# An output projection done in three parts instead of two, two of them beside attention

## The chip, the cores and the metric

The kernel runs on one core of a Trainium2 chip. The metric is the device time of one execution in microseconds (us). Engines are called by their names: TensorE (PE in the profile, its weight loads PEld), VectorE (DVE), ScalarE (ACT), GpSimd (POOL), and SyncE (SP), whose queue issues most of the transfers.

## The reference

Two layers of a hybrid backbone work on 256 context tokens and 1024 latent tokens of 1024 features. Each layer normalises its input, projects it into the inputs of four mixers (S5, mLSTM, differential attention, gated linear attention or GLA), joins their four outputs of 256 features, projects them, and adds the result to its input through a gate. An MLP with squared ReLU follows. In the second layer only the latent tokens go on.

```python
s5 = s5_mixer(zc[0], zl[0], p, need_ctx)
ml = mlstm_mixer(zc[1:6], zl[1:6], p, need_ctx)
da = diff_attention_mixer(zc[6:9], zl[6:9], p, layer_idx, need_ctx)
gl = gla_mixer(zc[9:14], zl[9:14], p, need_ctx)
mix_l = jnp.concatenate([s5[1], ml[1], da[1], gl[1]], axis=-1) @ p['w_out']
x_lat = x_lat + g1 * mix_l
hl2 = rms_norm(x_lat, p['norm2_g']) * (1.0 + sc2) + sh2
x_lat = x_lat + g2 * sq_relu_mlp(hl2, p['mlp_w1'], p['mlp_w2'])
```

The same is done for the context tokens in the first layer, with their own gates.

## The kernel before

Features lie on partitions and tokens in the free dimension. The 1280 tokens form three blocks: block 0 holds the 256 context tokens, blocks 1 and 2 hold 512 latent tokens each. Products of full precision are made of three matmuls (`mm3`, lines 1128 to 1130): both operands are split into a high and a low part, and high times high, high times low and low times high are summed. In each layer S5 and GLA run first, beside the input projections, and write their outputs to `mix_d` in DRAM, a buffer of four mixers by two row blocks of 128 features.

Then comes the attention stage. Three generators are interleaved by hand. `da_mix` is attention: per head and query tile, scores on TensorE (`daps`), their maxima and copies on VectorE (`das`, line 489), the exponential on ScalarE (line 500), the combination of two maps on VectorE (line 508), transposes (`dapt`) and value products (`dapo`) on TensorE. It has 372 steps in layer 0 and 340 in layer 1 (counted in the code: a latent head has 85, a head's context part 8). `ml_mix` is mLSTM, with 90 and 80 steps. `p_out` is the first part of the output projection: rows of S5 and GLA (`MIX[0]`), in pieces of 256 tokens, 8 output blocks m each, so 40 steps in layer 0 and 32 in layer 1. `both(da, 1, ml, 0.25)` takes one mLSTM step for every four attention steps, and `beside(..., po, 0.12)` gives the projection 0.12 steps for each attention step.

A step of `p_out` loads a piece of the layer's input (`xo`), takes 12 matmuls into one PSUM bank (`wop`), scales them by the gate on ScalarE (`pg`, line 1484), adds on GpSimd (line 1485) and stores the sum to `xn_d`. The weights are split once, in the first piece of tokens (lines 1459 to 1461), stored to `wsp` in DRAM, and loaded from there afterwards (`whl`, two buffers). `mix_parts` loads and splits the mixer outputs (`mr`, `mh`, `ml`). The banks of `wop` and of attention's transposes have the same tag in this stage, with two buffers.

In the tail, X is loaded from `xn_d`, and the rows of mLSTM and attention (`MIX[1]`) are projected block by block, 512 tokens at a time, in the order of `LAST`: blocks 1, 2, 0 in layer 0, and 1, 2 in layer 1. Each m takes 4 x 3 matmuls, then line 1530 adds the result to X on VectorE. Squares of X and their sums (`nsq` on ScalarE, `np` on TensorE) follow, and `norm_block` makes the MLP's input from three operations per feature block (lines 1212 to 1214). Then the MLP starts.

Of the kernel before, what the change touches and what calls it, by code (L numbers as in the profile page):

```python
# [12 lines left out]
F32 = mybir.dt.float32  # L13
F32R = mybir.dt.float32r
# [9 lines left out]
T = 1280  # L24
# [1073 lines left out]
BLK = [(0, 256), (256, 768), (768, 1280)]  # L1098
# [2 lines left out]
ZORD = ["dak1 dak2 daq1 daq2 s50 s51 ga glk glq glv glr0 glr1 dav mlk0 mlk1 mlq0 mlq1 mlv mlo".split(),  # L1101
        "s50 s51 dak1 dak2 daq1 daq2 ga glk glq glv glr0 glr1 dav mlk0 mlk1 mlq0 mlq1 mlv mlo".split()]
BANKS = dict(z="m", ada="o", nm="b", s5p="a", s5v="a", s5y="o", s5z="b", das="a", dat="b", das2="x", dao="p", gls="a", glo="b", mls="o", mlv="m", wo="m")
MIX = ((0, 3), (1, 2))
FIRST = ((0, 1, 2), (1, 2, 0))
LAST = ((1, 2, 0), (1, 2))
LAT_ONLY = {"mlq0", "mlq1", "daq1", "daq2", "glq", "mlo", "glr0", "glr1"}
# [16 lines left out]
def mm3_steps(pe, out, pairs):  # L1124

    n = len(pairs)
    for i, ((ah, al), (bh, bl)) in enumerate(pairs):
        pe.matmul(out, ah, bh, start=i == 0, stop=False)  # L1128
        pe.matmul(out, ah, bl, start=False, stop=False)  # L1129
        pe.matmul(out, al, bh, start=False, stop=i == n - 1)  # L1130
        yield 3 * out.shape[-1]


def mm3(pe, out, pairs):
    for _ in mm3_steps(pe, out, pairs):
        pass


def beside(main, filler, rate, guard=contextlib.nullcontext):

    credit = 0.0
    for c in main:
        credit += rate * c
        if credit > 0:
            with guard():
                while credit > 0:
                    credit -= next(filler, 1e9)
# [69 lines left out]
def both(a, na, b, nb):  # L1217

    ca = cb = 0.0
    for x in a:  # L1220
        yield x
        ca += 1
        while cb / nb < ca / na:
            next(b, None)
            cb += 1
# [44 lines left out]
def tile_hybrid_backbone(ctx: ExitStack, tc: tile.TileContext, io, out):  # L1270
    nc = tc.nc
    env = Env()
# [44 lines left out]
    def mod(l, part, s):  # L1317
        return mods[l][:, 8 * part:8 * part + 8, s]

    def pool(nm, side=None):  # L1320
        p = tc.tile_pool(name=nm, bufs=1, side=side, reuse_waits="tile") if side else tc.tile_pool(name=nm, bufs=1, reuse_waits="tile")
        return p, p.__enter__()

    def shut(p):
        p.__exit__(None, None, None)
# [42 lines left out]
    for l in range(L):  # L1368
# [8 lines left out]
        if l == 0:  # L1377

            npc, P = pool("nx0", "right")
# [28 lines left out]
        def put(i):  # L1408
            def cb(m, t, c0):
                (nc.sync, nc.scalar, nc.sync, nc.sync)[i].dma_start(mix_d[i, m, :, c0:c0 + t.shape[1]], t)  # L1410
            return cb
# [3 lines left out]
        if l == 0:  # L1415
            ready(("dak1",))
            spc, P = pool("s5p0")
# [17 lines left out]
        shut(wpc)  # L1435
        blocks = range(3) if need else range(1, 3)
        x_d = io["xT"] if l == 0 else xl_d
        xn_d = env.dram.tile([128, 8, T], F32, name=f"xn{l}", tag=f"xn{l}")
        xl_d = env.dram.tile([128, 8, T], F32, name=f"xl{l}", tag=f"xl{l}")

        def mix_parts(P, t0, n, z, w=512):

            mh = P.tile([128, 4, w], F32R, tag="mh", name="mh", bufs=1)
            ml_ = P.tile([128, 4, w], F32R, tag="ml", name="ml", bufs=1)
            for k in range(4):
                mr = env.wp.tile([128, 512], F32, tag="zst", name="mr", bufs=2)
                nc.sync.dma_start(mr[:, :n], mix_d[MIX[z][k // 2], k % 2, :, t0:t0 + n])
                nc.scalar.copy(mh[:, k, :n], mr[:, :n])
                nc.vector.tensor_tensor(ml_[:, k, :n], mr[:, :n], mh[:, k, :n].bitcast(F32), op=ALU.subtract)
            return [(mh[:, k, :n], ml_[:, k, :n]) for k in range(4)]  # L1450

        wsp = [env.dram.tile([8, 128, 2, 512], F32, name=f"wsp{z}{l}", tag=f"wsp{z}{l}") for z in range(2)]

        def out_proj(m, n, z, parts, first):

            w = env.wp.tile([128, 2, 512], F32R, tag="whl", name="whl", bufs=env.whl)
            if first:
                raw = env.wp.tile([128, 512], F32, tag="raw", name="raw", bufs=2)
                nc.sync.dma_start(raw.rearrange("p (i y) -> p i y", y=256), io["wo"][l, m].rearrange("p (i y) -> p i y", y=256)[:, MIX[z][0]:MIX[z][1] + 1:MIX[z][1] - MIX[z][0]])
                nc.scalar.copy(w[:, 0], raw)  # L1460
                nc.vector.tensor_tensor(w[:, 1], raw, w[:, 0].bitcast(F32), op=ALU.subtract)
                nc.sync.dma_start(wsp[z][m], w.bitcast(F32))
            else:
                nc.sync.dma_start(w.bitcast(F32), wsp[z][m])
            wh, wl = (w[:, i].rearrange("p (k c) -> p k c", k=4) for i in range(2))
            p = env.bank("wo", "wop")
            mm3(nc.tensor, p[:, :n], [((wh[:, k], wl[:, k]), parts[k]) for k in range(4)])
            return p[:, :n]

        def p_out(P):  # L1470

            w = 256
            for b in blocks:
                t0, t1 = BLK[b]
                for c in range(t0, t1, w):
                    n = min(w, t1 - c)
                    g1 = mod(l, 2, b == 0)
                    parts = mix_parts(P, c, n, 0, w)
                    for m in range(8):
                        x = P.tile([128, w], F32, tag="xo", name="xo", bufs=2)  # L1480
                        nc.sync.dma_start(x[:, :n], x_d[:, m, c:c + n])
                        p = out_proj(m, n, 0, parts, c == BLK[blocks[0]][0])
                        pg = P.tile([128, w], F32, tag="pg", name="pg", bufs=1)
                        nc.scalar.mul(pg[:, :n], p, g1[:, m:m + 1])
                        nc.gpsimd.tensor_tensor(x[:, :n], x[:, :n], pg[:, :n], op=ALU.add)
                        nc.sync.dma_start(xn_d[:, m, c:c + n], x[:, :n])
                        yield n / 256
# [3 lines left out]
        wpc, env.wp = pool("wpd")  # L1491
        env.whl = 2
        poc, P = pool(f"po{l}")
        po = p_out(P)
        da = da_mix(env, l, st, zd["dav"], io["da_lam"][l], 0.8 - 0.6 * math.exp(-0.3 * l), io["da_ng"][l], env.bones, put_da, need)
        mgc, MG = pool(f"mlg{l}", "right")
        mgates = ml_gates(env, l, MG, zd["gates"], io["ml_gb"][l], io["amask"], io["hsel"])
        ml = ml_mix(env, l, mgates, lambda i: zd[("mlq0", "mlq1", "mlk0", "mlk1")[i]], zd["mlv"], zd["mlo"], io["ml_cw"][l], io["ml_cb"][l],
                    io["ml_ng"][l], io["cmask"], put(1), need)
        beside((1 for _ in both(da, 1, ml, 0.25)), po, 0.12)  # L1500
        list(ml)
        shut(mgc)
        list(po)
        env.banks.update(BANKS)
        shut(ps2c)
        ps2c = banks(f"ps2{l}")
# [8 lines left out]
        for b in blocks:  # L1515
            n = BLK[b][1] - BLK[b][0]
# [3 lines left out]
        woc, P = pool(f"wo{l}", "right")  # L1520
        env.wp = P
        parts = None
        for i, b in enumerate(LAST[l]):
            n = BLK[b][1] - BLK[b][0]
            s = 1 if b == 0 else 0
            parts = parts or mix_parts(P, BLK[b][0], n, 1)
            g1 = mod(l, 2, s)
            for m in range(8):
                p = out_proj(m, n, 1, parts, i == 0)
                nc.vector.scalar_tensor_tensor(X[b][:, m], p, g1[:, m:m + 1], X[b][:, m], op0=ALU.mult, op1=ALU.add)  # L1530
            if i + 1 < len(LAST[l]):
                b1 = LAST[l][i + 1]
                parts = mix_parts(P, BLK[b1][0], BLK[b1][1] - BLK[b1][0], 1)
            norm_block(env, P, X[b], block_rstd(env, P, X[b], n), n, scl[l][:, 1, s], mod(l, 3, s), *H[b])
        shut(woc)
        env.wp = wp
# [4 lines left out]
        hdc, P = pool(f"hid{l}", "right")  # L1541
# [6 lines left out]
        def acc(nm):  # L1548
            turn[0] += 1
            env.banks["mlp"] = "mb"[turn[0] % 2]  # L1550
            return env.bank("mlp", nm)

        def split_side(src):
            for gen, every in side:
                if steps[0] % every == 0:
                    next(gen, None)
            steps[0] += 1
            return split_w(env, src, 1024)
# [8 lines left out]
        for g in range(32 // G):  # L1567
            hid = []
            for f in range(G):
                wh, wl = (w.rearrange("p (k c) -> p k c", k=8) for w in split_side(io["w1"][l, G * g + f]))  # L1570
                hhi = P.tile([128, T], F32R, tag="hhi", name="hidhi", bufs=G + 1)
                hlo = P.tile([128, T], F32R, tag="hlo", name="hidlo", bufs=G + 1)
                for b in blocks:
                    t0, t1 = BLK[b]
                    n = t1 - t0
                    p = acc("m1p")
# [9 lines left out]
            if g < 32 // G - 1:  # L1586
                for i in range(G):
                    wh, wl = w2(i, split_side)
# [3 lines left out]
            else:  # L1592
# [26 lines left out]
    for b in blocks:  # L1619
        t0, t1 = BLK[b]  # L1620
        n = t1 - t0
        y = block_rstd(env, P, X[b], n)
# [94 lines left out]
```

## Time and profile before

| | us |
|---|---|
| median of 3 runs | 3681.51 |
| lowest and highest | 3678.64, 3687.2 |
| profiled execution, its own time | 3686.26 |
| its span in the profile | 3684.5 |

The span is the time from the first to the last recorded instruction; 1.8 us of the execution lie around it. The mean granted TensorE clock over the span is 0.955 of full speed. TensorE is busy 3393.9 us of the span, VectorE 2228.0, ScalarE 1309.5 and GpSimd 448.6. Busy times of TensorE hold the modelled ends of pipelined matmuls, so they are read beside the spacing of their starts.

### The profile page before, as it was taken

To read this page: it belongs to the slowest core of one execution; us is meant where nothing else is said; L and a number is where in the kernel's file an instruction comes from. 1 tells how busy PE (TensorE), PEld (TensorE's weight loads), DVE (VectorE), ACT (ScalarE), POOL (GpSimd) and SP (SyncE) were. 2 spreads that over 40 slices of the span, in tenths; PEclk is the share of its full clock that TensorE was granted. 3 is DMA by queue.
4 is the path that set the end of the run, shared out by engine and by line. 5 is a ranking of instruction groups with operands and counts; after the bars stand their busy time and mean duration, and the time that the engine had idled before them with its cause. 6 is when DMAs were issued, how large, how long until landed. Compare 5 with 4: busy or idle time off the path is not lost. (4 is left out here: it accounts for less than half of the span.)

```text
span 3684.5 us, 55377 instructions
## 1 busy us (share of the span) xinstructions
PE 3393.9 (92%) x21282; PEld 2677.8 (73%) x21282; DVE 2228.0 (60%) x5455; ACT 1309.5 (36%) x2457; POOL 448.6 (12%) x520
## 2 busy tenths in 40 slices
PE   6989998898789999999999798988889899999998
PEld 3767767676657888888888476867677578888885
DVE  9664785878659855555544647486888543333334
ACT  4223434666542121212111522444776422122222
POOL 2131221223100000000000113130222000000000
PEclk8989999898899999999999898999999899999999
DMA  6775314655461222222111365314654511111112
GB/s 220 238 221 155 119 68 143 211 181 169 146 205 58 90 83 76 85 76 76 64 41 38 110 197 163 111 66 141 219 175 126 191 41 46 52 46 52 46 49 77
DMA packets 233966, 430.36 MB, mean 117 GB/s; under 512 B 47414, under 2 KB 135910, under 8 KB 233446
## 3 DMA queue, kind: packets, MB, share of 16 engines
q1 hardware_dynamic: 192806, 381.03, 31.7%
q10 hardware_dynamic: 35520, 30.52, 2.6%
q0 software_dynamic: 5376, 15.28, 1.2%
q8 instruction: 168, 2.75, 0.3%
q14 instruction: 96, 0.79, 0.1%
HBM read 316.88 MB, written 109.86 MB: 116 GB/s over the span
## 5 line engine op out<-in xcount | busy, mean ns | idle before, releaser
L1566 DVE SCALAR_TENSOR_TENSOR X<-m2p,mods,X 128x256 f32<-128x256 f32 (+1 forms) x512 | 344.9, 682 | 345.5 <-PE m2p L1130 344.9
L1119 ACT CAST whi<-raw 128x1024 fp32r<-128x1024 f32 x182 | 191.1, 1050 | 919.7 <-PE m2p L1129 640.8
L1128 PE MATMUL m2p<-hidhi,whi 128*128 128x512 f32 (+1 forms) x1280 | 473.4, 372 | 3.1 <-DVE X L1566 2.4
L1130 PE MATMUL m2p<-hidhi,wlo 128*128 128x512 f32 (+1 forms) x1280 | 472.0, 370 | 0.8 <-DVE wlo L1120 0.8
L1128 PE MATMUL m1p<-h2hi,whi 128*128 128x512 f32 (+1 forms) x1280 | 472.6, 370 | 0.2 <-ACT h2hi L1213 0.2
L1129 PE MATMUL m2p<-hidlo,whi 128*128 128x512 f32 (+1 forms) x1280 | 472.7, 369 | 0.0
L1129 PE MATMUL m1p<-h2lo,whi 128*128 128x512 f32 (+1 forms) x1280 | 471.0, 368 | 0.0
L1130 PE MATMUL m1p<-h2hi,wlo 128*128 128x512 f32 (+1 forms) x1280 | 470.9, 368 | 0.0
L1120 DVE TENSOR_TENSOR wlo<-raw,whi 128x1024 fp32r<-128x1024 f32 x182 | 224.5, 1234 | 315.2 <-ACT whi L1119 302.7
L1128 PEld LDWEIGHTS m2p<-hidhi,whi 128*128 128x128 f32 x1280 | 241.3, 189 | 60.4 <-issue 9.4
L1128 PEld LDWEIGHTS m1p<-h2hi,whi 128*128 128x128 f32 x1280 | 241.0, 188 | 46.5 <-ACT whi L1119 4.2
L1130 PEld LDWEIGHTS m2p<-hidhi,wlo 128*128 128x128 f32 x1280 | 241.0, 188 | 46.4 <-issue 3.4
L1129 PEld LDWEIGHTS m2p<-hidlo,whi 128*128 128x128 f32 x1280 | 241.4, 189 | 41.8 <-issue 2.2
L1129 PEld LDWEIGHTS m1p<-h2lo,whi 128*128 128x128 f32 x1280 | 241.2, 188 | 40.6 <-DVE h2lo L1214 0.6
L1130 PEld LDWEIGHTS m1p<-h2hi,wlo 128*128 128x128 f32 x1280 | 241.0, 188 | 40.2 <-issue 0.4
L1128 PE MATMUL zp<-hhi,whi 128*128 128x512 f32 (+1 forms) x664 | 254.5, 384 | 11.3 <-ACT zst L1241 9.6
L1129 PE MATMUL zp<-hlo,whi 128*128 128x512 f32 (+1 forms) x664 | 251.4, 379 | 8.6 <-DVE hlo L1209 8.2
L489 DVE TENSOR_SCALAR_CACHE_REDUCE das<-daps 128x512 f32<-128x512 f32 (+1 forms) x400 | 225.8, 587 | 45.5 <-PE daps L488 42.9
L1130 PE MATMUL zp<-hhi,wlo 128*128 128x512 f32 (+1 forms) x664 | 250.0, 377 | 0.0
L1580 DVE TENSOR_TENSOR rl<-rl,m1p 128x256 f32<-128x256 f32 (+1 forms) x160 | 100.6, 629 | 172.2 <-ACT rl L1579 172.1
L500 ACT ACTIVATE das<-das,danm 128x1280 f32<-128x1280 f32 x128 | 174.3, 1362 | 48.1 <-DVE danm L498 47.9
L488 PE MATMUL daps<-daqk,daqk 128*128 128x512 f32 (+1 forms) x400 | 149.7, 438 | 41.3 <-DVE das L489 39.8
(460 smaller groups left out, 6571.9 us busy)
## 6 DMA issues: line engine op xcount, KB each, us to landing
raw<-w SPq DMA_DIRECT2D x136, 512.0 KB
adaw<-ada_w SPq DMA_DIRECT2D x96, 512.0 KB
whl<-wsp SPq DMA_DIRECT2D x80, 512.0 KB
wsp<-whl SPq DMA_DIRECT2D x32, 512.0 KB
raw<-wz SPq DMA_DIRECT2D x30, 512.0 KB
daqk<-da_st SPq DMA_DIRECT2D x24, 640.0 KB
mlE<-ml_rows SPq DMA_DIRECT2D x16, 640.0 KB
xn<-xo SPq DMA_DIRECT2D x72, 128.0 KB
```

What stands on the lines that cost most here:

```text
L488: pe.matmul(p[:, 0:b - a], Q[m][:, 128 * qt:128 * qt + 128], K[m][:, a:b], start=True, stop=True)
L489: v.tensor_scalar(s[:, a:b], p[:, 0:b - a], -1.0, None, op0=ALU.mult, op1=ALU.min, accum_out=pm[:, i:i + 1])
L500: act.activation(s[:, :k1], s[:, :k1], AF.Exp, bias=nm[:, 0:1], scale=-1.0, accum_out=sm[m])
L1119: nc.scalar.copy(hi, raw)
L1120: nc.vector.tensor_tensor(lo, raw, hi.bitcast(F32), op=ALU.subtract)
L1128: pe.matmul(out, ah, bh, start=i == 0, stop=False)
L1129: pe.matmul(out, ah, bl, start=False, stop=False)
L1130: pe.matmul(out, al, bh, start=False, stop=i == n - 1)
L1566: nc.vector.scalar_tensor_tensor(X[b][:, m], p[:, :n], mod(l, 5, s)[:, m:m + 1], X[b][:, m], op0=ALU.mult, op1=ALU.add)
L1580: nc.vector.tensor_tensor(rl[:, :n], rl[:, :n], p[:, :n], op=ALU.mult)
```

## The change

The output projection is cut into three parts: `MIX` becomes (S5, GLA), (mLSTM), (attention). The first part runs beside attention and mLSTM, as before, at 0.2 steps per attention step, and mLSTM at 0.43; after `SPLIT` steps of attention (210 in layer 0, 190 in layer 1) what is left of mLSTM and of the first part is finished. The second part, mLSTM's rows with half as many matmuls per step, runs beside the rest of attention at 0.25. It reads the first part's sums from a new buffer `xm_d` and writes `xn_d`. The tail is left with attention's rows.

```diff
-MIX = ((0, 3), (1, 2))
+MIX = ((0, 3), (1,), (2,))
+SPLIT = (210, 190)
...
+        xm_d = env.dram.tile([128, 8, T], F32, name=f"xm{l}", tag=f"xm{l}")
...
         def mix_parts(P, t0, n, z, w=512):
+            nk = 2 * len(MIX[z])
...
-            for k in range(4):
+            for k in range(nk):
...
-        wsp = [env.dram.tile([8, 128, 2, 512], F32, name=f"wsp{z}{l}", tag=f"wsp{z}{l}") for z in range(2)]
+        wsp = [env.dram.tile([8, 128, 2, 256 * len(MIX[z])], F32, name=f"wsp{z}{l}", tag=f"wsp{z}{l}") for z in range(3)]
...
-            w = env.wp.tile([128, 2, 512], F32R, tag="whl", name="whl", bufs=env.whl)
+            nk = 2 * len(MIX[z])
+            w = env.wp.tile([128, 2, 512], F32R, tag="whl", name="whl", bufs=env.whl)[:, :, 0:128 * nk]
...
-            mm3(nc.tensor, p[:, :n], [((wh[:, k], wl[:, k]), parts[k]) for k in range(4)])
+            mm3(nc.tensor, p[:, :n], [((wh[:, k], wl[:, k]), parts[k]) for k in range(nk)])
...
-        def p_out(P):
+        def p_out(P, z, x_d, xn_d):
...
-        po = p_out(P)
+        po = [p_out(P, 0, x_d, xm_d), p_out(P, 1, xm_d, xn_d)]
...
-        beside((1 for _ in both(da, 1, ml, 0.25)), po, 0.12)
+        beside((1 for _ in itertools.islice(both(da, 1, ml, 0.43), SPLIT[l])), po[0], 0.2)
         list(ml)
         shut(mgc)
-        list(po)
+        list(po[0])
+        beside((1 for _ in da), po[1], 0.25)
+        list(po[1])
...
-            parts = parts or mix_parts(P, BLK[b][0], n, 1)
+            parts = parts or mix_parts(P, BLK[b][0], n, 2)
...
-                p = out_proj(m, n, 1, parts, i == 0)
+                p = out_proj(m, n, 2, parts, i == 0)
```

## Rows read from the trace of the kernel before

**Rows 1.** The page: busy us, share of the span, instructions.
```profile
PE 3393.9 (92%) x21282; PEld 2677.8 (73%) x21282; DVE 2228.0 (60%) x5455; ACT 1309.5 (36%) x2457; POOL 448.6 (12%) x520
```

**Rows 2.** Windows: us, busy PE, PEld, DVE, ACT, POOL, PE clock, DMA share, GB/s.
```profile
648.00:1002.00 354.00, 306.08 (x2606) 237.29 (x2605) 277.21 (x932) 229.02 (x514) 83.06 (x78) 0.90 0.53 174
...
1015.00:1105.00 90.00, 80.98 (x337) 49.91 (x338) 50.97 (x79) 38.11 (x65) 0.00 (x0) 0.97 0.60 204
2565.00:2874.00 309.00, 266.57 (x2284) 206.34 (x2286) 252.16 (x815) 212.78 (x445) 75.38 (x64) 0.91 0.55 179
...
2888.00:2953.00 65.00, 59.96 (x206) 35.01 (x206) 33.59 (x48) 24.62 (x40) 0.00 (x0) 0.93 0.55 182
```

**Rows 3.** Two windows of 30 us in layer 0's attention stage, same columns.
```profile
820.00:850.00 30.00, 18.48 (x171) 13.13 (x169) 23.89 (x68) 19.25 (x50) 10.32 (x5) 0.76 0.38 128
...
880.00:910.00 30.00, 29.23 (x267) 22.49 (x267) 23.99 (x89) 19.62 (x44) 10.16 (x8) 1.00 0.62 192
```

**Rows 4.** Waits, VectorE and SP, layer 0: us in total, times, longest us.
```profile
DVE das L489 <- PE daps L488: 27.7, 31, 3.0
...
SPq L1486 <- POOL xo L1485: 85.9, 35, 8.2
```

**Rows 5.** Line 1530 in either tail, and what it waited for (us, times).
```profile
L1530 DVE SCALAR_TENSOR_TENSOR X<-wop,mods,X x24: 476/750/752, 1017.8 to 1104.2; 128x512 f32<-128x512 f32 x16, 128x256 f32<-128x256 f32 x8
...
  PE wop L1130: 23.3, 13
...
L1530 DVE SCALAR_TENSOR_TENSOR X<-wop,mods,X x16: 744/750/752, 2890.4 to 2952.1; 128x512 f32<-128x512 f32 x16
...
  PE wop L1130: 22.4, 11
```

**Rows 6.** Timeline of VectorE in layer 0's tail: start us, us, what.
```profile
1043.84 0.75 DVE L1530 SCALAR_TENSOR_TENSOR X<-wop,mods,X 128x512 f32<-128x512 f32 x1 [1.97 <-PE wop L1130]
...
1051.16 1.28 DVE L1449 TENSOR_TENSOR ml<-mr,mh 128x512 fp32r<-128x512 f32 x2
...
1053.42 0.74 DVE L1530 SCALAR_TENSOR_TENSOR X<-wop,mods,X 128x512 f32<-128x512 f32 x1
...
1070.64 0.75 DVE L1530 SCALAR_TENSOR_TENSOR X<-wop,mods,X 128x512 f32<-128x512 f32 x1 [1.85 <-PE wop L1130]
1074.57 0.75 DVE L1530 SCALAR_TENSOR_TENSOR X<-wop,mods,X 128x512 f32<-128x512 f32 x1 [3.18 <-PE wop L1130]
```

**Rows 7.** Timeline of TensorE in layer 0's tail.
```profile
1021.04 0.40 PE L1129 MATMUL wop<-ml,whl 128*128 128x512 f32 x1
...
1024.47 0.39 PE L1129 MATMUL wop<-ml,whl 128*128 128x512 f32 x1
...
1070.54 1.04 PE L1187 MATMUL np<-nsq,ones 128*32 128x512 f32 x2
1071.51 0.50 PE L1128 MATMUL wop<-mh,whl 128*128 128x512 f32 x1
...
1090.06 0.28 PE L1130 MATMUL wop<-mh,whl 128*128 128x256 f32 x1
...
1092.10 0.28 PE L1129 MATMUL wop<-ml,whl 128*128 128x256 f32 x1
```

**Rows 8.** Groups by line and shape, layer 0's attention stage: busy us, mean ns.
```profile
L1484 ACT ACTIVATE pg<-wop,mods 128x256 f32<-128x256 f32 x40 | 18.8, 471 | 32.4 <-PE wop L1130 28.1 <-POOL xo L1485 3.9
...
L1449 DVE TENSOR_TENSOR ml<-mr,mh 128x256 fp32r<-128x256 f32 x20 | 8.0, 417 | 1.0 <-ACT mh L1448 1.0
```

**Rows 9.** Windows of the two attention stages, instructions of `wop` alone (PE, PEld, DVE, ACT).
```profile
648.00:1002.00 354.00, 80.98 (x480) 69.01 (x480) 0.00 (x0) 18.84 (x40) 0.90 0.53 174
...
2565.00:2874.00 309.00, 62.84 (x384) 54.46 (x384) 0.00 (x0) 15.08 (x32) 0.91 0.55 179
```

**Rows 10.** DMA issues in layer 0's attention stage: count, KB each.
```profile
X<-xn SPq DMA_DIRECT2D x2, 2048.0 KB
...
X<-xn SPq DMA_DIRECT2D x1, 1024.0 KB
```

More of the change, by code (lines that the diff above doesn't have):

```diff
@@ L4 @@
 import contextlib
+import itertools
 from concourse import mybir
@@ L1449, in mix_parts @@
                 nc.vector.tensor_tensor(ml_[:, k, :n], mr[:, :n], mh[:, k, :n].bitcast(F32), op=ALU.subtract)
-            return [(mh[:, k, :n], ml_[:, k, :n]) for k in range(4)]
-        wsp = [env.dram.tile([8, 128, 2, 512], F32, name=f"wsp{z}{l}", tag=f"wsp{z}{l}") for z in range(2)]
+            return [(mh[:, k, :n], ml_[:, k, :n]) for k in range(nk)]
+        wsp = [env.dram.tile([8, 128, 2, 256 * len(MIX[z])], F32, name=f"wsp{z}{l}", tag=f"wsp{z}{l}") for z in range(3)]
         def out_proj(m, n, z, parts, first):
-            w = env.wp.tile([128, 2, 512], F32R, tag="whl", name="whl", bufs=env.whl)
+            nk = 2 * len(MIX[z])
+            w = env.wp.tile([128, 2, 512], F32R, tag="whl", name="whl", bufs=env.whl)[:, :, 0:128 * nk]
             if first:
-                raw = env.wp.tile([128, 512], F32, tag="raw", name="raw", bufs=2)
-                nc.sync.dma_start(raw.rearrange("p (i y) -> p i y", y=256), io["wo"][l, m].rearrange("p (i y) -> p i y", y=256)[:, MIX[z][0]:MIX[z][1] + 1:MIX[z][1] - MIX[z][0]])
+                raw = env.wp.tile([128, 512], F32, tag="raw", name="raw", bufs=2)[:, 0:128 * nk]
+                nc.sync.dma_start(raw.rearrange("p (i y) -> p i y", y=256), io["wo"][l, m].rearrange("p (i y) -> p i y", y=256)[:, MIX[z][0]:MIX[z][-1] + 1:max(1, MIX[z][-1] - MIX[z][0])])
                 nc.scalar.copy(w[:, 0], raw)
@@ L1464, in out_proj @@
                 nc.sync.dma_start(w.bitcast(F32), wsp[z][m])
-            wh, wl = (w[:, i].rearrange("p (k c) -> p k c", k=4) for i in range(2))
+            wh, wl = (w[:, i].rearrange("p (k c) -> p k c", k=nk) for i in range(2))
             p = env.bank("wo", "wop")
-            mm3(nc.tensor, p[:, :n], [((wh[:, k], wl[:, k]), parts[k]) for k in range(4)])
+            mm3(nc.tensor, p[:, :n], [((wh[:, k], wl[:, k]), parts[k]) for k in range(nk)])
             return p[:, :n]
-        def p_out(P):
+        def p_out(P, z, x_d, xn_d):
             w = 256
@@ L1477, in p_out @@
                     g1 = mod(l, 2, b == 0)
-                    parts = mix_parts(P, c, n, 0, w)
+                    parts = mix_parts(P, c, n, z, w)
                     for m in range(8):
@@ L1481, in p_out @@
                         nc.sync.dma_start(x[:, :n], x_d[:, m, c:c + n])
-                        p = out_proj(m, n, 0, parts, c == BLK[blocks[0]][0])
+                        p = out_proj(m, n, z, parts, c == BLK[blocks[0]][0])
                         pg = P.tile([128, w], F32, tag="pg", name="pg", bufs=1)
@@ L1532, in tile_hybrid_backbone @@
                 b1 = LAST[l][i + 1]
-                parts = mix_parts(P, BLK[b1][0], BLK[b1][1] - BLK[b1][0], 1)
+                parts = mix_parts(P, BLK[b1][0], BLK[b1][1] - BLK[b1][0], 2)
             norm_block(env, P, X[b], block_rstd(env, P, X[b], n), n, scl[l][:, 1, s], mod(l, 3, s), *H[b])
```

## The prediction

> **What bounds the kernel now.** I read the page's busy shares first, then the windows, the waits, the groups by line and the timelines. TensorE is busy 92% of the span [rows 1], but most of that is input projection and MLP, which the change leaves alone. It works in two stretches of each layer, so those are read by themselves [rows 2]. The attention stage of layer 0 runs from 648 to 1002 us (354 us), of layer 1 from 2565 to 2874 (309 us). The tail, in which the second half of the output projection is done, carries on to 1105 and 2953: 90 us and 65 us after the last attention block has arrived.
>
> In the attention stage no engine is full. TensorE shows 306 of 354 us, VectorE 277, ScalarE 229; in layer 1 it is 267, 252 and 213 of 309 [rows 2]. TensorE's share overstates it: ends of matmuls are modelled, and of two windows of 30 us one has it at 29.2 and the other at 18.5, and VectorE works 24.0 and 23.9 in them [rows 3]. The longest wait of VectorE is for the score matmuls, 27.7 us over 31 times [rows 4], so the stage is a pipeline of three engines that take turns, VectorE the densest of those with honest durations: 0.783 of the stage in layer 0 and 0.816 in layer 1.
>
> In the tail it is plainer. VectorE works 51 of 90 us, and its update of X waits for the projection's matmuls 23.3 us over 13 times in layer 0 and 22.4 us over 11 times in layer 1 [rows 2, 5]. In steady state one output block m takes 3.93 us (X at 1070.64 and 1074.57) [rows 6]. That is 12 matmuls of 512 columns, 0.229 us apart (15 steps from 1021.04 to 1024.47), so 2.74 us, and 0.97 us of norm matmuls (1070.54 to 1071.51), 3.7 us together [rows 7]. The tail is TensorE's.
>
> **The change part by part.** (1) *Removed from the tail*: the two mLSTM row blocks, 6 of the 12 matmuls of each m. An m then costs 6 x 0.229 + 0.97 = 2.34 us, 1.37 less. VectorE needs about 2.2 us per m where X and the norm of the block before meet (three operations on 128x512, each taken at the 0.74 us of X [rows 6]), so TensorE and VectorE come out level and nearly all of the 1.37 us is real. Block 1 of layer 0: X runs from 1017.8 to 1043.84, seven periods of 3.72 us [rows 5, 6]; 7 x 1.37 = 9.6, less some 1.4 us because mLSTM matmuls of the first two m's are now done while the last attention block is still on its way: 8.2. Between blocks, X stands still from 1043.84 to 1053.42: four input pieces have to be split, in two pairs, the second only at 1051.16 [rows 6]. With two pieces that second pair is gone. Block 2 then needs its 8 x 2.34 = 19 us behind a shorter gap, but VectorE still has the norm of block 1 to do (from 1053.4, 16 operations and the X updates left over, about 14 us), so it ends near 1068 and not at 1079: 10 us rather than 14. The last block of 256 columns (0.12 us a matmul, 17 steps from 1090.06 to 1092.10 [rows 7]) is VectorE's more than TensorE's: 4 us. Layer 0: 22 us. Layer 1 has blocks 1 and 2 alone, at the same prices: 8 + 8 = 16. **Tail: -38 us.** Its upper end is every removed matmul at its spacing, 192 x 0.229 + 48 x 0.12 = 49.7 us; its lower end is half of what X waits for now, 23 us.
>
> (2) *Added to the attention stage*: 40 steps in layer 0 and 32 in layer 1. A step is 6 matmuls of 256 columns (0.12 us apart, 0.72 us), one scaling on ScalarE (0.471 us, 19 + 15 us in all), one add on GpSimd (its engine has 83 of 354 us, nothing waits), and three transfers on SP's queue: the x piece, the weight piece, and the store of the sum into the new buffer. Beside them stand 18 input splits (10 and 8, 0.417 us on VectorE) and 16 weight splits at half width, for which the 256-wide split is the nearest row [rows 8]. VectorE therefore gets 18 x 0.417 = 7.5 us in layer 0 and 16 x 0.417 = 6.7 in layer 1. At the density that the stage has now this is 7.5 / 0.783 + 6.7 / 0.816 = 17.8 us. **Stage: +18 us.** From below, nothing, if matmuls and splits fall into the gaps that exist. From above, the matmuls pay their whole place: at their issue spacing 432 x 0.12 = 52 us; at the busy time that a projection matmul shows in this stage now (81.0 us / 480 and 62.8 / 384, 0.169 and 0.164 us [rows 9]) 240 x 0.169 + 192 x 0.164 = 72 us. I take the VectorE figure because the stage waits around VectorE, and the room beside it (TensorE's weight loads fill 237 of 354 us [rows 2]) holds 29 us of matmuls.
>
> (3) *Moved*: the mLSTM steps go from 0.25 to 0.43 per attention step and the first part from 0.12 to 0.2, so both are over after 210 of the 372 attention steps (190 of 340 in layer 1); the rest of attention has only the second part beside it. The amount of work is unchanged, so I cost it at nothing; what hides it is that VectorE's density hardly moves between windows, whether mLSTM's heavy steps fall into them (820 to 850) or not [rows 3]. If that cover fails, the first stretch is the crowded one. SP already waits 85.9 us in the stage for the GpSimd add before it can issue a store [rows 4], with weight loads, key loads and decay rows queued behind; with the first part at 0.2 these come closer together.
>
> (4) *Late at the seam*: the final sum of the last 256 tokens is now stored at the very end of attention, where it used to be over 40 steps earlier. X is loaded from it in two pieces of 2 MB and one of 1 MB [rows 10]; one of 2 MB at the end delays the small loads of the last attention outputs on the same queue: +3 us, an estimate (0 to 12). A few adaptive-norm matmuls of the next layer that now lie in the tail move on into the MLP: +2 us.
>
> The rows show 0.229 us for 512 columns and 0.12 for 256 [rows 7], so cutting the mLSTM half into 256-wide pieces costs 5% more issue time: 52 us for what takes 49.7 in the tail. The Trainium skill, "Perfetto Trace Analysis", Optimizing Tensor Performance, speaks against this part: larger matmuls are more efficient than smaller ones where they are possible. The trace agrees, but only by those 2 us; the sum is the same by the rule and by the rows.
>
> **Sum**, against the profiled execution's own 3686.3 us (span 3684.5, 1.8 around it): -38 + 18 + 3 + 2 = -15, so 3671. That execution lies 4.8 us over the median of the runs, 3681.5; the median forecast is 3666 us.
>
> **Rivals.** *Full price in the stage.* TensorE is the stage's limit, as windows with 29.2 of 30 us suggest [rows 3]. Place: the issue slots of TensorE, in which the attention scores wait behind the projection. Then +52 for +18: -38 + 52 + 5 = +19, 3700 us. It decides from 33 us of stage cost on, where the tail's gain is gone. For it: VectorE's longest wait is for those scores [rows 4]. Against: weight loads fill only 67% of the stage.
>
> *All hidden.* The stage takes the new work for nothing: -38 + 5 = -33, 3648 us. For it: VectorE gets only 14 us. Against: three engines already take turns, and each new step occupies all of them. The Trainium skill, "Perfetto Trace Analysis", Identifying the Most-Contended Engine, says that matmul busy time is no measure of TensorE's room and that the weight-load share is; by it full price is out and VectorE is the engine to count, and the two rows of [rows 3] agree.
>
> *Gain eaten by the crowding.* The first stretch, with mLSTM and the first part pressed into 210 steps, loses another 15 us through SP's queue and buffers: net 0, 3681 us. For it: the SP wait [rows 4]. Against: the transfers average 174 GB/s at a DMA share of 0.53 in the stage [rows 2].
>
> **How the numbers follow.** The forecast (3650 to 3677) has 0.52, all hidden 0.15, crowding 0.13, full price 0.20. About 0.2%, 7 us, is what a measurement of this kernel can tell from no change, so faster is below 3674. Faster: most of the forecast (0.45) and all hidden, 0.60. Within: the forecast's upper edge 0.06, crowding 0.10, full price's lower edge 0.03, 0.19. Slower: 0.17 of full price, 0.03 of crowding and 0.01 of the forecast, 0.21. The range reaches from below all hidden (3638, tail near its upper end) to inside full price (3693).
>
> **What would show it.** Tail: X every 2.3 to 2.6 us instead of 3.9, no second pair of splits between blocks, first to last X in layer 0 down from 86 us to about 64. Stage: 18 us longer over both layers together, VectorE near 0.8 of it; TensorE's granted clock in it, now 0.90 and 0.91 [rows 2], not lower. Seam: the last X load behind the last attention store. I am wrong if the two stages grow by over 33 us, if VectorE's density falls in the first stretch, or if the tail's period stays above 3 us because a weight piece, with two buffers, arrives later than 2.3 us after its buffer is free.

## The result and the profile after

The changed kernel takes 3817.2 us (median of 4 runs, 3810.96 to 3832.17), the kernel before 3680.07 beside it: a ratio of 1.0375, 95% interval 1.034 to 1.0409. It is 137 us slower; 3666 was forecast, in a range that ended at 3693. Below, 1% is 36.8 us, and every ratio is against the kernel before run on the same chip.

The page of the changed kernel shows each engine with a little more work, to be compared with [rows 1].

```profile
PE 3447.9 (91%) x21474; PEld 2712.1 (71%) x21474; DVE 2242.0 (59%) x5479; ACT 1349.3 (35%) x2553; POOL 503.5 (13%) x592
```

No engine has more than 55 us added (GpSimd 55, TensorE 54, ScalarE 40, VectorE 14), so the 137 us are not the added work of any one of them. The windows tell where they lie (columns as in [rows 2]): first the two attention stages whole, each with its tail, then each stage cut where the second part begins.

```profile
648.00:1091.00 443.00, 362.52 (x2846) 279.89 (x2846) 293.29 (x948) 253.22 (x568) 112.02 (x116) 0.86 0.60 190
1095.00:1165.00 70.00, 57.46 (x214) 30.43 (x215) 46.93 (x75) 35.11 (x61) 0.00 (x0) 0.93 0.54 174
2630.00:3025.00 395.00, 325.15 (x2490) 246.97 (x2490) 264.95 (x836) 236.40 (x497) 95.29 (x96) 0.88 0.60 187
3030.00:3080.00 50.00, 42.90 (x124) 19.66 (x124) 30.26 (x46) 23.70 (x40) 0.00 (x0) 0.90 0.46 148
...
645.00:910.00 265.00, 226.07 (x1916) 179.33 (x1918) 189.63 (x619) 153.85 (x369) 78.42 (x74) 0.86 0.63 200
910.00:1091.00 181.00, 138.50 (x938) 101.92 (x938) 105.56 (x338) 101.32 (x207) 35.02 (x44) 0.86 0.57 177
...
2630.00:2880.00 250.00, 214.81 (x1732) 166.54 (x1732) 181.77 (x582) 152.63 (x338) 67.95 (x64) 0.86 0.61 195
2880.00:3025.00 145.00, 110.34 (x758) 80.43 (x758) 83.18 (x255) 83.76 (x159) 27.34 (x33) 0.90 0.56 174
```

The windows grew from 354 to 443 and from 309 to 395 us. They are cut by eye, so here are the last outputs of attention in layer 0 and layer 1, before and after (first and last start, us):

```profile
L556 DVE SCALAR_TENSOR_TENSOR dao<-dao,ng,rs_y x8: 340/700/746, 679.7 to 1005.7; 128x128 f32<-128x128 f32 x4, 128x512 f32<-128x512 f32 x4
L556 DVE SCALAR_TENSOR_TENSOR dao<-dao,ng,rs_y x4: 739/746/752, 2675.0 to 2881.9; 128x512 f32<-128x512 f32 x4
...
L557 DVE SCALAR_TENSOR_TENSOR dao<-dao,ng,rs_y x8: 339/542/752, 679.4 to 1091.1; 128x128 f32<-128x128 f32 x4, 128x512 f32<-128x512 f32 x4
L557 DVE SCALAR_TENSOR_TENSOR dao<-dao,ng,rs_y x4: 736/865/1046, 2768.5 to 3024.9; 128x512 f32<-128x512 f32 x4
```

The first score matmuls start at 648.1 and 2571.1 us before and at 645.8 and 2634.3 after. From there to the last output the stages grew by 87.7 and 79.8 us. VectorE worked 0.783 and 0.816 of the windows [rows 2]; now it is 293.29 / 443 = 0.66 and 264.95 / 395 = 0.67. It is 0.72 in the first stretch and 0.58 in the second of layer 0 (189.63 / 265, 105.56 / 181). No other engine took its place: TensorE and ScalarE are less dense too, and GpSimd works a quarter of the time. TensorE's granted clock is 0.86 and 0.88 in the two stages, where it was 0.90 and 0.91 [rows 2]. The tail did what was asked of it. These are the update of X in layer 0 and layer 1, answering to [rows 5]:

```profile
L1537 DVE SCALAR_TENSOR_TENSOR X<-wop,mods,X x24: 480/750/755, 1099.7 to 1162.8; 128x512 f32<-128x512 f32 x16, 128x256 f32<-128x256 f32 x8
...
  PE wop L1132: 13.0, 13
...
L1537 DVE SCALAR_TENSOR_TENSOR X<-wop,mods,X x16: 744/751/752, 3033.5 to 3076.8; 128x512 f32<-128x512 f32 x16
...
  PE wop L1132: 11.5, 8
```

From first to last X it takes 63.1 us in layer 0 (86.4 before) and 43.3 (61.7), and the waits for matmuls are halved. Stages and tails together make 87.7 + 79.8 - 23.3 - 18.4 = 125.8 us, and the spans of the two profiled executions differ by 124.7 (3809.2 against 3684.5). VectorE's timeline there answers to [rows 6]:

```profile
1099.71 0.75 DVE L1537 SCALAR_TENSOR_TENSOR X<-wop,mods,X 128x512 f32<-128x512 f32 x1 [1.31 <-PE wop L1132]
1100.99 0.75 DVE L1537 SCALAR_TENSOR_TENSOR X<-wop,mods,X 128x512 f32<-128x512 f32 x1 [0.20 <-PE wop L1132]
...
1116.47 0.75 DVE L1537 SCALAR_TENSOR_TENSOR X<-wop,mods,X 128x512 f32<-128x512 f32 x1 [0.61 <-PE wop L1132]
1117.14 1.28 DVE L1453 TENSOR_TENSOR ml<-mr,mh 128x512 fp32r<-128x512 f32 x2
...
1142.74 0.75 DVE L1453 TENSOR_TENSOR ml<-mr,mh 128x256 fp32r<-128x256 f32 x2
```

Between blocks there is one pair of splits, no longer two. So the loss is in the attention stage. In its second stretch (layer 0) these waits of GpSimd, VectorE and ScalarE are new or have grown (in the whole stage before, their totals were 6.8, 1.4, 6.4 and 3.9 us); columns are total us, times, longest:

```profile
POOL xo L1490 <- DMA xo<-xm: 64.3, 18, 8.0
...
DVE das L490 <- PE dapt L530: 21.8, 4, 8.8
...
DVE dao L551 <- ACT dao L550: 14.7, 2, 14.5
ACT pg L1489 <- POOL xo L1490: 11.9, 10, 2.0
```

GpSimd's timeline in the same stretch shows the adds of the second part:

```profile
1000.72 0.73 POOL L1490 TENSOR_TENSOR xo<-xo,pg 128x256 f32<-128x256 f32 x1 [4.34 <-DMA xo<-xm]
1002.67 0.73 POOL L1490 TENSOR_TENSOR xo<-xo,pg 128x256 f32<-128x256 f32 x1 [1.22 <-DMA xo<-xm]
...
1013.55 0.79 POOL L1490 TENSOR_TENSOR xo<-xo,pg 128x256 f32<-128x256 f32 x1 [4.36 <-DMA xo<-xm]
```

An add waits for its x piece, the one buffer of the scaled result waits for the add, ScalarE waits for that buffer, the PSUM bank for ScalarE, and attention's transposes, which use the same two banks, for the bank. That was the first theory (R): the second part's round trip through its buffers holds attention up. Its rival (P): the moved pacing costs by itself.

### The profile page after: what moved, and what is told of

Its sections match the earlier page's. It is cut to its first block, busy times and chain, and to the rows that moved or that the text cites. A ratio compares the mean times of both kernels' runs of the same rounds, so it can differ in the third digit from the quotient of the medians.

```text
span 3809.2 us, 56498 instructions
## 1 busy us (share of the span) xinstructions
PE 3447.9 (91%) x21474; PEld 2712.1 (71%) x21474; DVE 2242.0 (59%) x5479; ACT 1349.3 (35%) x2553; POOL 503.5 (13%) x592
## 5 line engine op out<-in xcount | busy, mean ns | idle before, releaser
L1130 PE MATMUL wop<-mh,whl 128*128 128x256 f32 (+1 forms) x512 | 183.1, 360 | 67.7 <-DMA whl<-wsp 29.4
L489 PE MATMUL daps<-daqk,daqk 128*128 128x512 f32 (+1 forms) x400 | 159.5, 464 | 45.6 <-DVE das L490 43.3
```

The lines of the kernel that those rows point to most:

```text
L489: pe.matmul(p[:, 0:b - a], Q[m][:, 128 * qt:128 * qt + 128], K[m][:, a:b], start=True, stop=True)
```

## The experiments

**The change taken apart.** The first pair splits the loss into three. One kernel has the new pacing and the old two parts:

```diff
-MIX = ((0, 3), (1,), (2,))
+MIX = ((0, 3), (1, 2))
...
-        beside((1 for _ in da), po[1], 0.25)
-        list(po[1])
+        list(da)
```

> The old two parts (S5 and GLA beside attention, attention and mLSTM in the tail), with the change's pacing (0.43, 0.2, SPLIT) and nothing beside the rest of attention. Theory R (the second part's round trip through its buffers holds attention up; the pacing is harmless): about the time of the kernel before, 3680 to 3705 us. Theory P (the pacing itself costs: mLSTM is the cover under which attention's waits lie, and the rest of attention is left without it): 3740 us or more, both stages longer by 30 us or more each with no second part in them, VectorE's busy share after 930 us of layer 0 below 0.5.

Measured: 3745.8 us, 1.0159 (1.013 to 1.0189). The other leaves the mLSTM part out of the changed kernel, so its output lacks that contribution:

```diff
-        po = [p_out(P, 0, x_d, xm_d), p_out(P, 1, xm_d, xn_d)]
+        po = [p_out(P, 0, x_d, xn_d)]
...
-        beside((1 for _ in da), po[1], 0.25)
-        list(po[1])
+        list(da)
```

> The changed kernel with the mLSTM part of the projection left out altogether (its output lacks mLSTM's contribution), everything else in place. Against the run with the pacing alone it shows the tail's gain by itself: both theories expect 30 to 45 us less than that run. Against the changed kernel it prices the second part: theory R expects 3650 to 3670 us, so that the second part costs 150 us; theory P expects 3710 to 3780, so that it costs 40 to 100.

Measured: 3713.54 us, 1.0077 (1.0054 to 1.0099). So the pacing costs 1.59% (58 us), the smaller tail gives 0.82% (30 us) back, and the second part costs 1.0375 - 1.0077 = 2.98% (110 us); the intervals of the three ratios are 8 to 13 us either way. Neither theory is enough alone: theory P has the total of the first run right and its place wrong. The windows of the run with the pacing alone:

```profile
645.00:940.00 295.00, 247.05 (x2096) 194.14 (x2097) 221.04 (x722) 173.28 (x404) 80.94 (x77) 0.88 0.62 201
940.00:1000.00 60.00, 52.78 (x384) 36.88 (x382) 54.34 (x176) 44.30 (x85) 0.00 (x0) 0.97 0.18 59
```

Attention by itself is not slow: VectorE works 54.34 of 60 us, 0.91, against 0.78 for the whole stage before. The time is lost in the first stretch, at 221.04 / 295 = 0.75. The Trainium skill, "Perfetto Trace Analysis", Optimization Strategy, says that where the most-contended engine changes over time, interleaving the regimes may help. The new pacing draws them apart, and that it cost 1.59% goes with the rule; but in the first stretch the rows show no engine that is full.

**The second part's waits.** Two edits to the changed kernel, one for each link of theory R. The second part's results go into the banks that mLSTM has left:

```diff
+        env.banks.update(wo="m")
         beside((1 for _ in da), po[1], 0.25)
```

> The changed kernel with the second part's PSUM results in the two banks that mLSTM has left, not in the two that it shares with the transposed attention weights. Theory R in the form that the shared banks tie attention to the second part's chain: 40 to 80 us faster than the changed kernel (3740 to 3775). If only the SP and GpSimd chain or the pacing matters: within 15 us of 3817.

Measured: 3786.93 us, 1.0278 (1.0258 to 1.0298), 0.97% or 36 us less than the changed kernel, a little under what theory R asked. The x pieces are loaded two steps ahead, and the scaled result gets a second buffer:

```diff
+        x = P.tile([128, w], F32, tag="xo", name="xo", bufs=4 if z else 2)
...
+    xs = [fetch(0), fetch(1)] if z else []
     for m in range(8):
+        if not z or m < 6:
+            xs.append(fetch(m + 2 * z))
+        x = xs.pop(0)
...
-        pg = P.tile([128, w], F32, tag="pg", name="pg", bufs=1)
+        pg = P.tile([128, w], F32, tag="pg", name="pg", bufs=2 if z else 1)
```

> The changed kernel with the second part's x pieces loaded two steps ahead into four buffers and two buffers for its scaled result, in the room that mLSTM has left. The 34 waits of GpSimd for that load (119 us in the whole run) should all but vanish. Theory R in the form that this load is the slow link: 40 to 90 us faster than the changed kernel (3730 to 3775). Theory P: within 20 us of it.

Measured: 3800.36 us, 1.0313 (1.0293 to 1.0333): 0.62%, 23 us. The waits for the piece are gone, as this row of its second stretch shows, but most of the time is not back:

```profile
POOL xo L1497 <- ACT pg L1496: 115.5, 36, 16.0
POOL xo L1497 <- DMA xo<-xm: 3.1, 1, 3.1
```

The bank is the dearer link. The Trainium skill, "Perfetto Trace Analysis", Optimizing Tensor Performance, asks that independent matmul groups rotate through PSUM banks so that eviction overlaps the next group; here two streams shared two banks, and separating them gave the 36 us. Both edits and four weight buffers together (the loosened kernel, below):

```diff
+        env.banks.update(wo="m")
...
+            w = (env.pq if z == 1 else env.wp).tile([128, 2, 512], F32R, tag="whl", name="whl", bufs=4 if z == 1 else env.whl)[:, :, 0:128 * nk]
```

> The changed kernel with everything of the second part loosened at once: results in the two banks that mLSTM left, x pieces loaded two steps ahead into four buffers, two buffers for the scaled result, four weight buffers. The second part costs 2.9% (110 us) in the changed kernel; the banks alone gave back 1.0%, the loads alone 0.6%. If its cost is waits (round trip and banks): 2.2% or more back, 1.010 to 1.018 of before, near the run without a second part (1.008). If it is work that the attention stage has no room for (TensorE issue, VectorE): 1.6% back or less, 1.022 or more.

Measured: 3767.89 us, 1.0226 (1.0195 to 1.0257). That is 1.49% (55 us) back, and as much of the second part's price is left. By the expectation that is the second outcome, work that finds no room; two runs below test it. First the round trip left out, all else as in the changed kernel (the output lacks mLSTM's contribution):

```diff
+                        if not z:
+                            x = P.tile([128, w], F32, tag="xo", name="xo", bufs=2)
+                            nc.sync.dma_start(x[:, :n], x_d[:, m, c:c + n])
...
+                        if not z:
+                            nc.gpsimd.tensor_tensor(x[:, :n], x[:, :n], pg[:, :n], op=ALU.add)
+                            nc.sync.dma_start(xn_d[:, m, c:c + n], x[:, :n])
```

> The changed kernel whose second part stops after the scaling: its x loads, GpSimd adds and stores are left out (the output lacks mLSTM's contribution), the weight and input loads, splits, matmuls, shared banks and scalings stay. If the round trip through DRAM, SP's queue and GpSimd carries the cost: 1.008 to 1.018 of before. If matmuls, banks and weight pieces carry it: 1.025 to 1.037.

Measured: 3781.55 us, 1.0277 (1.0252 to 1.0302): 0.98%, 36 us. So the round trip carries a third of the price, and matmuls, banks and weight pieces the rest. Is the rest TensorE's place? The loosened kernel with half of the second part's matmuls:

```diff
-            mm3(nc.tensor, p[:, :n], [((wh[:, k], wl[:, k]), parts[k]) for k in range(nk)])
+            mm3(nc.tensor, p[:, :n], [((wh[:, k], wl[:, k]), parts[k]) for k in range(1 if z == 1 else nk)])
```

> The loosened kernel (own banks, loads ahead, more buffers; 1.0226 of before, so that its second part costs 55 us) with 3 of the 6 matmuls of each step of the second part left out (half of mLSTM's contribution is missing). 216 matmuls are gone, 26 us at their issue spacing. If what is left of the second part's cost is TensorE's place: 20 to 30 us less, 1.014 to 1.017. If it is waits, transfers or VectorE: within 8 us, 1.020 to 1.025.

Measured: 3760.85 us, 1.0209 (1.0192 to 1.0226), 0.17% (6 us) under the loosened kernel, with intervals of 6 and 11 us either way. Most of their issue time of 26 us is not in it, so TensorE's work is at most a part of what is left. In the loosened kernel's second stretch TensorE does wait for its weights:

```profile
PEld wop L1130 <- DMA whl<-wsp: 7.3, 10, 1.5
PE wop L1130 <- DMA whl<-wsp: 6.8, 8, 1.7
```

The next run keeps the eight weight pieces in the room that mLSTM left, instead of storing them and loading them again for each piece of tokens (the expectation counts these loads too high: there are 32 in layer 0 and 24 in layer 1):

```diff
+            w = (env.pq.tile([128, 2, 256], F32R, tag="wk", name="whk", bufs=8) if first else env.kept[m]) if z == 1 else env.wp.tile(...)
```

> The loosened kernel (1.0226 of before) whose second part keeps its eight weight pieces in the room that mLSTM left, so that 64 loads of 256 KB a layer less eight first ones are gone (TensorE waited for such a piece 6.8 us in 100 us of the second stretch). If these loads are what is left of the second part's price: 0.7% or more less, 1.009 to 1.016. If the price is in the scalings and in engines that take turns: within 0.3%, 1.020 to 1.026.

Measured: 3749.11 us, 1.0165 (1.015 to 1.018): another 0.61% (22 us), most of what was expected if these loads were the rest. Over the kernel without a second part (1.0077) 0.88% is left, 32 us for 72 steps. With the stores moved to GpSimd's queue as well:

```diff
-                        nc.sync.dma_start(xn_d[:, m, c:c + n], x[:, :n])
+                        (nc.gpsimd if z else nc.sync).dma_start(xn_d[:, m, c:c + n], x[:, :n])
```

> The run before this one, with the second part's stores issued by GpSimd, right behind its own add, so that no load on SP's queue stands behind a store that waits for the add. If SP's order still holds the second part: another 0.5% or more less than with the weights kept alone. If not: within 0.3% of it.

Measured: 3751.09 us, 1.0176 (1.0154 to 1.0197), no gain. But the edit did not take the wait off SP. Between 930 and 1056 us SP had waited 43.1 us for the add and 11.6 us, before the next x load, for a store to leave its buffer; now it waits 68.9 us for the latter. Whether SP's order is a link is not told by this run.

**The pacing.** Two runs with the old two parts, one edit of the pacing each:

```diff
-        beside((1 for _ in itertools.islice(both(da, 1, ml, 0.43), SPLIT[l])), po[0], 0.2)
+        beside((1 for _ in both(da, 1, ml, 0.43)), po[0], 0.12)
```

> The old two parts, mLSTM at 0.43 steps per attention step as in the change, the first part at its old 0.12 over all of attention. The pacing alone cost 1.6% (58 us). Theory M (mLSTM pressed into 210 of 372 steps is what crowds the first stretch): 1.0% or more slower than before still, 3720 to 3745. Theory F (the first part at 0.2, its SP and GpSimd traffic, is what crowds it): within 0.4% of before.

Measured: 3721.62 us, 1.0111 (1.0096 to 1.0126).

```diff
+        beside((1 for _ in both(da, 1, ml, 0.25)), po[0], 0.2)
```

> The counterpart: mLSTM at its old 0.25, the first part at 0.2 beside all of it, old two parts. Theory M: within 0.4% of before (3670 to 3700). Theory F: 1.0% or more slower. If both runs lie near half, 0.6 to 1.0% each, it is the two together.

Measured: 3747.87 us, 1.0181 (1.0164 to 1.0198). None of the outcomes expected came: each pacing costs over 1% by itself, and the first part at 0.2 alone as much as the whole new pacing. The prices do not add up (1.1 + 1.8 against 1.6). A likely reason, which was not tried, is that the two together leave a stretch with attention alone, in which VectorE catches up (0.91 in the rows above). To see what the first part costs at 0.12, it was left out of the kernel before (its output lacks S5 and GLA):

```diff
-        po = p_out(P)
+        po = iter(())
...
-            nc.sync.dma_start(X[b], xn_d[:, :, BLK[b][0]:BLK[b][1]])
+            nc.sync.dma_start(X[b], x_d[:, :, BLK[b][0]:BLK[b][1]])
```

> The kernel before with its first part left out whole (the output lacks the S5 and GLA contribution); attention and mLSTM at their old 0.25, tail as it was. It prices the 72 steps of 12 matmuls that the attention stage carried already; at their issue spacing they are 104 us. If the stage has TensorE gaps that take projection work for little: 20 to 50 us less than before (0.986 to 0.995). If every projection matmul pays its whole place: 85 to 120 us less (0.967 to 0.977).

Measured: 3642.56 us, 0.9886 (0.9871 to 0.9901). At 0.12 the 72 steps cost 1.14%, 42 us, 0.58 us a step, where their matmuls alone take 1.44 us to issue: the stage does take them into its gaps. (The granted clock over the span was 0.941 to 0.945 without them and 0.955 to 0.958 in the kernel before beside it, so what the clock took is in the 42 us.) At 0.2 the same steps cost 1.0181 - 0.9886 = 2.95%, 109 us, 1.5 us a step. What makes density dear? Four runs, each with the first part at 0.2 and mLSTM at 0.25, and one thing taken from it. Its round trip (no x loads, adds, stores; X from the layer's input):

```diff
-                        x = P.tile([128, w], F32, tag="xo", name="xo", bufs=2)
-                        nc.sync.dma_start(x[:, :n], x_d[:, m, c:c + n])
...
-                        nc.gpsimd.tensor_tensor(x[:, :n], x[:, :n], pg[:, :n], op=ALU.add)
-                        nc.sync.dma_start(xn_d[:, m, c:c + n], x[:, :n])
```

> The kernel with the first part at 0.2 and mLSTM at its old 0.25 (1.018 of before), and the first part's round trip left out: no loads of x, no GpSimd adds, no stores of sums; X is loaded from the layer's input (the output lacks the S5 and GLA contribution). Weight pieces, input splits, matmuls and scalings stay. If the round trip through two x buffers and SP's queue is what makes a denser first part dear: 0.990 to 1.004. If it is the matmuls and their banks in between attention's: 1.010 to 1.018.

Measured: 3715.38 us, 1.0092 (1.0075 to 1.0109), 0.89% less. Between the two outcomes expected. The stores on GpSimd's queue, and the same edit to the kernel before as its control:

```diff
-                        nc.sync.dma_start(xn_d[:, m, c:c + n], x[:, :n])
+                        nc.gpsimd.dma_start(xn_d[:, m, c:c + n], x[:, :n])
```

> The first part at 0.2 and mLSTM at 0.25 (1.018 of before), with the stores issued by GpSimd. If a step's loads behind the store of the step before are what makes the denser first part dear: 0.7% or more less, 1.000 to 1.011. If it is the steps' work between attention's: 1.015 to 1.020.

> The kernel before, its first part's stores issued by GpSimd instead of SP; everything else as it was. SP waited 85.9 us for the add in the stage of layer 0. If SP's order costs time at the old density of 0.12 too: 0.4% or more faster than before (0.985 to 0.996). If the first part has slack there: 0.997 to 1.004.

Measured: 1.0203 (1.0186 to 1.022) and 1.0015 (1.0005 to 1.0024). No gain at either density. Here too the wait only moved. These are SP's waits in layer 0, ahead the two of the denser first part, then the one that is left with the stores moved:

```profile
SPq L1491 <- POOL xo L1490: 72.7, 37, 8.3
SPq L1486 <- DMA xn<-xo: 19.0, 14, 3.2
...
SPq L1486 <- DMA xn<-xo: 106.7, 28, 7.4
```

An x load needs the buffer that the store still holds, so it waits on SP in the store's place, 106.7 us for 91.7. The runs do not tell whether loads behind SP's waits make density dear. Half of the first part's matmuls:

```diff
-            mm3(nc.tensor, p[:, :n], [((wh[:, k], wl[:, k]), parts[k]) for k in range(nk)])
+            mm3(nc.tensor, p[:, :n], [((wh[:, k], wl[:, k]), parts[k]) for k in range(nk if z else 2)])
```

> The first part at 0.2 and mLSTM at 0.25, with 6 of the 12 matmuls of each step of the first part left out (GLA's contribution is missing); 432 matmuls, 52 us at their issue spacing. All transfers, splits, scalings and adds stay. If TensorE is what the dense stretch waits for: 0.8% or more less than 1.018, 1.000 to 1.010. If the weight pieces and the round trip are: 1.013 to 1.019.

Measured: 3731.91 us, 1.0141 (1.0117 to 1.0164): 0.40%, 15 us, for matmuls of 52 us issue time. The granted clock over the span fell beside it, from 0.947 to 0.949 to 0.940 to 0.943, so the 15 us are the matmuls' price less what the clock took. One weight piece for all steps, so no weight loads:

```diff
+            if z == 0 and not (first and m == 0):
+                w = env.one
```

> The first part at 0.2 and mLSTM at 0.25 (1.018 of before), with one weight piece, split once, used in all steps of the first part (its contribution is another matrix's). The weight loads, splits and stores of the first part are gone, 12 matmuls a step, input splits, scalings and the round trip of x stay. If the weight pieces make density dear: 1.000 to 1.009. If TensorE's place does: 1.013 to 1.019.

Measured: 3706.09 us, 1.0064 (1.004 to 1.0088): 1.17%, 43 us, the largest share. The splits and stores of seven weight pieces a layer went with the loads (on VectorE 14 x 0.69 = 10 us), and the granted clock rose to 0.954 to 0.957; both are in the 43 us. Windows of the same 120 us of layer 0: the kernel before, the denser first part, the denser first part with one weight piece, and the same without the round trip:

```profile
740.00:860.00 120.00, 103.38 (x897) 81.06 (x898) 96.62 (x317) 81.34 (x190) 28.48 (x29) 0.89 0.50 165
```

```profile
740.00:860.00 120.00, 110.69 (x908) 89.01 (x908) 80.18 (x267) 69.52 (x159) 30.41 (x32) 0.91 0.69 215
```

```profile
740.00:860.00 120.00, 105.57 (x929) 83.06 (x928) 95.20 (x299) 80.83 (x189) 34.51 (x34) 0.94 0.35 109
```

```profile
740.00:860.00 120.00, 114.94 (x1006) 92.99 (x1004) 78.99 (x273) 72.80 (x161) 10.95 (x13) 0.96 0.49 161
```

VectorE's work falls from 96.62 to 80.18 us and is 95.20 when the weight loads go, with 929 matmuls for 908; the DMA share goes 0.50, 0.69, 0.35. The share does not explain it: without the round trip it is 0.49, and VectorE has 78.99 us, in a kernel that is 0.89% faster. Nor does the granted clock, which is 0.89 in the kernel before and 0.91 with the denser first part. A window at fixed times also holds different steps in each kernel, so its density goes only roughly with the time. These are the weight loads in the same window of the kernel before and of the denser first part:

```profile
whl<-wsp SPq DMA_DIRECT2D x15, 512.0 KB
```

```profile
whl<-wsp SPq DMA_DIRECT2D x22, 512.0 KB
```

**Less dense on both sides?** The loosened kernel with its split after 290 (262) steps, mLSTM at 0.32, the first part at 0.145, the second at 0.5:

```diff
-SPLIT = (210, 190)
+SPLIT = (290, 262)
...
-        beside((1 for _ in itertools.islice(both(da, 1, ml, 0.43), SPLIT[l])), po[0], 0.2)
+        beside((1 for _ in itertools.islice(both(da, 1, ml, 0.32), SPLIT[l])), po[0], 0.145)
...
-        beside((1 for _ in da), po[1], 0.25)
+        beside((1 for _ in da), po[1], 0.5)
```

> The loosened kernel with the split later: mLSTM 0.32 and the first part 0.145 over 290 (262) attention steps, the second part at 0.5 beside the last 82 (78). If the pacing's 1.6% comes from the denser first stretch, it falls by more than half, and the second part's price stays near 55 us unless its own density costs in turn: 1.010 to 1.018. If the price rises with the density of projection steps wherever they stand, the second part gives the gain back: 1.020 to 1.030.

Measured: 3763.92 us, 1.0219 (1.02 to 1.0237), the same as the loosened kernel's 1.0226. What the first stretch gains, the second part, twice as dense, gives back: against the loosened kernel VectorE works 202.41 us for 194.01 between 645 and 910 us, and 99.58 for 116.95 between 910 and 1091. No version that does the whole computation beats the kernel before.

## Why the prediction was wrong

**The tail was right.** Step (1) gave -38; taken out alone the tail gave 30 us, from two ratios good to 8 and 11 us. The X spans shortened by 23.3 and 18.4 us where 22 and 16 were forecast (layer 1's second block was put at 8 and layer 0's at 10; at the same price layer 1 would have had 18). The period (2.39 us, seven of them from 1099.71 to 1116.47), the single pair of splits and the 64 us of layer 0 came as told. The seam of step (4), +5, was not measured by itself; it lies in the price of the second part.

**The step that failed first is (2), the stage at +18.** It counted the second part's matmuls, splits, scalings and adds, said of its three transfers only that they were on SP's queue, and of the add that nothing waits, though SP waits 85.9 us for it [rows 4] and ScalarE 3.9 [rows 8]. The part cost 110 us. 77 of them (1.0375 - 1.0165) went when its results had banks of their own, its loads ran ahead and its weights stayed, with all its matmuls, splits, scalings and adds still there. So they are not its arithmetic but the waits of a step that must fetch 256 KB of weights and 128 KB of x through two buffers every 3.7 us (38 x pieces between 940 and 1080 us). What is left, 32 us with the seam in it, lies within the bounds of the term, 0 and 52, but is nearly twice its 18; whether VectorE's density is its price is not shown. The step's waits had no price at all.

**The step that failed next is (3), moved work at nothing.** It cost 58 us. The cover named for it, VectorE's density hardly moving between windows, was read from two windows [rows 3] that both held projection steps at 0.12; it says nothing of windows with more. The text had the crowded first stretch as what is late if the cover fails, and as a rival at 15 us: the right place, at a quarter of its size. Whether it comes through SP's queue, as the text said, is open, for no run took SP's wait away.

**The rivals.** Full price was to be TensorE's issue slots. The total came out on its side, but its mechanism did not: half of the matmuls are worth 6 us of 26 in the second part and 15 of 52 in the first (at a lower clock). All hidden fell. Of the signs of being wrong, two came: the stages grew by 168 us, where 33 was the limit, and VectorE's density fell in the first stretch, 0.783 to 0.72. The third, a tail period above 3 us, did not. The granted clock of the stage, which was not to fall, fell to 0.86 and 0.88.

**What stays open.** The denser mLSTM alone costs 1.1%; which of its waits does it was not tried. The weight loads are 43 us of the denser first part, but TensorE waits for them by name 7.4 us at most between 700 and 860 us; whether they do harm as late weights, by making other transfers late, or behind SP's waits for buffers was not told apart. Nor was what the clock took or gave in the runs that leave work out. The shares at 0.2 were not measured at 0.12 too, so they are shares of the price there, not of its rise.

## What to carry to other kernels

A filler step has a price that depends on its spacing: the same 72 steps cost 0.58 us each at one per 8 attention steps and 1.5 at one per 5, so work that is moved to stand closer is not free even when no engine is full. Splitting an accumulation to move a part of it adds a load and a store of the running sum, and here, with shorter pieces of tokens, more loads of weights (32 and 24 of 256 KB); cost the bytes and the buffers of a new step before its arithmetic. To price a change of several parts, run the moved pacing with nothing in the new place, then leave the new work out: two runs gave all three terms here. And after an edit that moves a wait, read the same queue's waits again before calling the queue free.

## What the runs showed of the hardware

A wait can change its place without growing shorter. SP waited 85.9 us for GpSimd's add before it could issue a store [rows 4], and 36.4 us, before an x load, for a store to leave one of the two buffers. With the stores issued by GpSimd the first wait is gone, and the second takes over. These are its rows in layer 0 of the kernel before and of the run with the stores moved, which took 0.15% more time:

```profile
SPq L1481 <- DMA xn<-xo: 36.4, 24, 3.4
...
SPq L1481 <- DMA xn<-xo: 127.0, 33, 8.4
```

Neither the granted clock nor the DMA share says by itself how dense VectorE is. These are windows of the second stretch: the loosened kernel, the same with half of the second part's matmuls, and the kernel without a second part.

```profile
940.00:1030.00 90.00, 78.08 (x614) 61.95 (x611) 65.90 (x212) 66.59 (x136) 29.23 (x33) 1.00 0.76 236
```

```profile
940.00:1030.00 90.00, 76.22 (x499) 55.37 (x499) 68.47 (x217) 65.73 (x139) 30.20 (x34) 0.89 0.76 231
```

```profile
940.00:1030.00 90.00, 76.32 (x524) 54.09 (x525) 69.29 (x226) 60.30 (x112) 0.00 (x0) 0.85 0.09 28
```

VectorE works 65.90, 68.47 and 69.29 us of the 90, at a granted clock of 1.00 (the upper of the two levels, 2.4 GHz, throughout), 0.89 and 0.85 and a DMA share of 0.76, 0.76 and 0.09. What the clock is worth over the whole kernel these rows do not tell: the first is from the fastest of four executions, 3748 us at a mean clock of 0.953, where the other three took 3766 to 3772 at 0.946 to 0.949.
